# A hybrid convolution and retention block on one core: the MLP's combinations of its second weight moved beside its first product, and modulation products queued behind the rotary of k

## The chip, the cores and the metric

The kernel runs on 1 core of one Trainium2 chip. The metric is the device time of one execution, in microseconds (us).

## The reference

One layer acts on 2048 tokens of width 1024, all in float32. A conditioning vector c gives six vectors of 1024 (shift, scale and gate for either half of the layer).

```
mod = silu(c) @ w_ada + b_ada -> shift1, scale1, gate1, shift2, scale2, gate2
h   = rms_norm(x, g_pre_mix) * (1 + scale1) + shift1
xin, b_gate, c_gate, q, k, v, g = split(h @ w_in)
y_conv = b_gate * causal_conv3(c_gate * xin)
y_ret  = silu(g) * head_norm(retention(rotary(q), rotary(k), v))
x = x + gate1 * rms_norm(concat(y_conv, y_ret) @ w_out, g_post_mix)
h = rms_norm(x, g_pre_mlp) * (1 + scale2) + shift2
f = square(relu(h @ w_fc1)) @ w_fc2
x = x + gate2 * rms_norm(f, g_post_mlp)
```

## The kernel before

**Precision.** Every large product is made of three: both factors are split into a high part, cast by ScalarE, and a low part, subtracted by VectorE, and `mm3` (lines 141 to 144) issues high by high, high by low and low by high into one bank of PSUM.

**The mixer** takes the tokens in four blocks of 512 (b = 0 to 3). In each, `gemm_nat` and `gemm_t` run through the seven parts of `w_in` in the order V, K, G, Q, XIN, C, B and then through `w_out`, with weights of 128x1024 loaded, cast and subtracted by `wgroup` (lines 131 to 139, three buffers). Between them stand the rotary (lines 527 to 544: three VectorE operations on the bank, an addition on GpSimd), the transposes, the retention by tiles of 128 tokens (lines 619 to 660), the convolution, and the normalised input of the MLP of the block before (`h2_prep`). While one block runs, the next block's x is loaded and squared (`h1_scale`, line 238 and line 240) and its input made (`h1_tile`).

**Modulation.** `mod2(gi)` multiplies eight tiles of 128x1024 of `w_ada` (tiles "ada", line 416) by columns of silu(c) and sums them on VectorE into "wide" (lines 418 and 420). It is called for the first gate and the MLP's scale and gate after the part G of blocks 0, 1 and 2, and for the MLP's shift in block 0.

**The MLP** works on two halves of 1024 tokens (B = 0, 1), each product in Winograd's form of Strassen's method: seven products instead of eight, on quarter matrices and their combinations. `fc1` goes through 16 pairs of column tiles (t = 0 to 15, "rounds" below): four quarter weights of 256 KB are loaded (`quads`, line 801), GpSimd makes their four combinations (lines 890 to 893) for the sixth and later products, and seven quarter results leave to DRAM as "fd". `fc2` multiplies them by `w_fc2`, whose four combinations stand in DRAM as "w2d".

**The preparations.** `w2_prep(t)` (lines 496 to 504) makes those combinations for one t: it loads `w2[t]` as two tiles "w2r" of 512 KB (line 499), makes four subtractions in place on GpSimd (line 502) and stores four results of 256 KB (line 504). `w2_some(n)` makes the next n of the 16. It is called at lines 558, 697 and 722, all in the mixer.

**Buffers and order.** The tiles "x", "ada", "w2r", "row" and, in `fc2`, "fw" share one tag of three buffers (`x_tile`, line 86). A scheduler puts the instructions of each engine into one fixed order, which is kept on the chip; `tc.issue_after(i)` adds an edge that queues what is issued inside it behind i on i's engine. All DMAs are issued by SP.

Of the kernel before, what the change touches and what calls it, by code (L numbers as in the profile page):

```python
# [54 lines left out]
def block_kernel(  # L55
# [459 lines left out]
    with pa_stack:  # L515
# [11 lines left out]
        def rotary(ps, coss, sins, t, dst):  # L527
            pv = ps.rearrange("p (h s d) -> p h s d", h=H, s=2)
            qa = tmp()
            nc.vector.tensor_tensor(  # L530
                qa.rearrange("p (x d) -> p x d", d=HALF),
                ps.rearrange("p (x d) -> p x d", d=HALF),
                coss[:, t, :].unsqueeze(1).to_broadcast([P, 2 * H, HALF]),
                op=ALU.mult,
            )
            qb = tmp()
            qbv = qb.rearrange("p (h s d) -> p h s d", h=H, s=2)
            for s in range(2):
                nc.vector.tensor_tensor(
                    qbv[:, :, s, :], pv[:, :, 1 - s, :],  # L540
                    sins[:, t, s, :].unsqueeze(1).to_broadcast([P, H, HALF]),
                    op=ALU.mult,
                )
            nc.gpsimd.tensor_tensor(dst, qa, qb, op=ALU.add)

        for b in range(NB):
# [6 lines left out]
            for ps in vps:  # L553
                v_ = at("va")
                nc.scalar.copy(v_, ps)
                vs.append(v_)
            if b > 0:
                w2_some(2)
            coss, sins = rope_tables(b)
            kds = []  # L560

            def k_end(t, ps):
                kr = tmp()
                rotary(ps, coss, sins, t, kr)
                kd = at("vb")
# [5 lines left out]
                )  # L571
                kds.append(kd)

            if b == 0:
                for t in range(3):
                    k_end(t, kps[t])
                k_end(3, gemm_nat(w_in(KK), h_cur, KS, ALL[3:])[0])
            else:
                for t, ps in enumerate(gemm_nat(w_in(KK), h_cur, KS)):
                    k_end(t, ps)  # L580

# [5 lines left out]
            if b < 3:  # L587
                part = mod2((0, 2, 3)[b])
            kTs = []
# [104 lines left out]
            if b > 0:  # L694
                for _ in h2_prep(b - 1, h2_load(b - 1)):
                    pass
            w2_some(2 if b > 0 else 1)
            for j, ps in enumerate(gemm_t(w_in(BG), h_cur)):
# [13 lines left out]
            for ch, tag in enumerate(("kT", "sg")):  # L712
# [7 lines left out]
                if ch == 0:  # L720
                    if b < NB - 1:
                        w2_some(1)

# [150 lines left out]
    def fc1(B, hl, first, left=None, beside=None):  # L874
# [8 lines left out]
        for t in range(NP):  # L883
# [29 lines left out]
            relu2(f11, f11)  # L913
            nc.sync.dma_start(fd[B][1][t], f11)
            add(f12, prod(6), f12)
            step()
# [257 lines left out]
```

## Time and profile before

| | |
|---|---|
| median of 3 runs | 2238.92 us (2238.62 to 2243.34) |
| profiled execution | 2240.46 us, its span 2238.7 us |
| TensorE (PE), weight loads (PEld) busy | 2143.6 us (96%), 1765.9 us |
| VectorE (DVE), ScalarE (ACT), GpSimd (POOL) busy | 1442.8, 989.9, 586.7 us |
| mean granted TensorE clock | 0.988 |
| moved by DMA | 428.23 MB, mean 191 GB/s |
| loads of w2r | 32 of 512 KB, median 5.4 us to landing |

In the rows, a group of instructions stands with its line, engine, operation and tiles (out<-in, buffer numbers left out); busy time, a mean in ns; an idle time before it with its releaser, the instruction whose end let it go. "SPq" is SP's issuing of DMAs. PEclk is the granted share of TensorE's full clock. Matmuls overlap, so a mean of 390 ns does not say how often one starts. A transfer is busy on 16 DMA engines; "DMA share" is their mean.

### The profile page before, as it was taken

What the parts mean: (1) busy time and instruction counts of PE and PEld (TensorE: products, weight loads), DVE (VectorE), ACT (ScalarE), POOL (GpSimd) and SP (SyncE); (2) the same over time, 40 slices, a digit from 0 to 9 for tenths busy, and PEclk for the clock granted to TensorE, in tenths of its full rate; (3) what the DMA queues carried; (4) which work ended last, traced back from release to release, by engine and by line L of the source; (5) the groups of instructions that cost most, each with busy time, mean ns of one, the idle gap of its engine ahead of it and who ended that gap; (6) DMA issues with size and microseconds to landing.
All of it is one profiled execution on the core that took longest, in us unless ns stands there. A gap on an engine that the chain in (4) does not pass through costs nothing.

```text
span 2238.7 us, 28424 instructions
## 1 busy us (share of the span) xinstructions
PE 2143.6 (96%) x9736; PEld 1765.9 (79%) x9736; DVE 1442.8 (64%) x2198; ACT 989.9 (44%) x1714; POOL 586.7 (26%) x441
## 2 busy tenths in 40 slices
PE   3999999999999999989999999999999999999997
PEld 2787877878787888867888878888888888888885
DVE  7766845675567634776666687556776666555566
ACT  3332532244224522466555556444445555454453
POOL 4132254314423351243333300001433333010012
PEclk8999999999999999999999999999999999999999
DMA  7356467546655563566444477666764443666666
GB/s 283 132 179 220 157 229 242 177 143 214 212 174 202 182 229 129 200 209 217 150 151 148 135 231 219 204 194 192 259 229 155 150 154 120 211 190 197 196 191 242
DMA packets 197426, 428.23 MB, mean 191 GB/s; under 512 B 22560, under 2 KB 22560, under 8 KB 197280
## 3 DMA queue, kind: packets, MB, share of 16 engines
q1 hardware_dynamic: 197280, 426.41, 57.7%
q8 instruction: 76, 1.25, 0.2%
q14 instruction: 70, 0.57, 0.1%
HBM read 322.51 MB, written 103.81 MB: 190 GB/s over the span
## 4 chain that ended last, share of the span: by engine, by line
PE 67%; DMA 11%; issue 10%; DVE 7%; POOL 3%; ACT 1%; SPq 0%; DVEq 0%; POOLq 0%; ACTq 0%
PE g L142 20%; PE g L143 20%; PE g L144 20%; DMA w2r<-in_w 2%; DMA w2d<-w2r 2%; DMA fw<-fd 2%; PE m L142 2%; PE m L143 2%; PE m L144 2%; POOL w2r L502 2%; DMA ada<-in_ada 1%; DMA x<-in_x 1%; DVE pt L199 1%; DVE wl L807 1%; DVE ql L807 1%
## 5 line engine op out<-in xcount | busy, mean ns | idle before, releaser
L143 PE MATMUL g<-ql,wh 128*128 128x512 f32 x896 | 350.9, 392 | 9.6 <-DVE ql L807 9.6
L144 PE MATMUL g<-qh,wl 128*128 128x512 f32 x896 | 350.9, 392 | 0.5 <-DVE wl L807 0.4
L142 PE MATMUL g<-qh,wh 128*128 128x512 f32 x896 | 350.2, 391 | 0.1
L136 ACT CAST whi<-raw 128x1024 fp32r<-128x1024 f32 x148 | 155.3, 1052 | 348.5 <-PE g L144 178.4
L872 DVE TENSOR_TENSOR q<-g,q 128x512 f32<-128x512 f32 x267 | 178.4, 687 | 174.8 <-PE g L144 174.6
L138 DVE TENSOR_TENSOR wlo<-raw,whi 128x1024 fp32r<-128x1024 f32 x140 | 187.6, 1344 | 152.2 <-ACT whi L136 151.7
L807 DVE TENSOR_TENSOR fl<-fw,fh 128x512 fp32r<-128x512 f32 x218 | 161.3, 741 | 162.5 <-ACT fh L806 160.3
L143 PE MATMUL g<-wl,fh 128*128 128x512 f32 x680 | 265.3, 390 | 0.3 <-DVE wl L807 0.3
L144 PE MATMUL g<-wh,fl 128*128 128x512 f32 x680 | 264.6, 389 | 0.0
L806 ACT CAST fh<-fw 128x512 fp32r<-128x512 f32 x218 | 135.2, 620 | 225.8 <-DMA fw<-fd 213.1
L806 ACT CAST wh<-r 128x512 fp32r<-128x512 f32 x224 | 138.8, 620 | 214.7 <-PE g L143 188.7
L142 PE MATMUL g<-wh,fh 128*128 128x512 f32 x680 | 218.4, 390 | 0.8 <-ACT wh L806 0.8
L143 PEld LDWEIGHTS g<-ql,wh 128*128 128x128 f32 x896 | 169.0, 189 | 46.6 <-DVE ql L807 11.5
L144 PEld LDWEIGHTS g<-qh,wl 128*128 128x128 f32 x896 | 169.1, 189 | 36.3 <-DVE wl L807 1.9
L142 PEld LDWEIGHTS g<-qh,wh 128*128 128x128 f32 x896 | 169.3, 189 | 36.1 <-ACT qh L806 0.7
L807 DVE TENSOR_TENSOR wl<-fw,wh 128x512 fp32r<-128x512 f32 x218 | 156.2, 717 | 44.7 <-ACT wh L806 42.2
L1005 POOL TENSOR_TENSOR q<-q,gg 128x512 f32<-128x512 f32 x28 | 43.4, 1577 | 533.4 <-ACT q L1002 285.3
L807 DVE TENSOR_TENSOR wl<-r,wh 128x512 fp32r<-128x512 f32 x224 | 163.6, 731 | 11.0 <-ACT wh L806 10.8
L806 ACT CAST wh<-fw 128x512 fp32r<-128x512 f32 x218 | 135.0, 619 | 65.3 <-PE g L144 30.3
L890 POOL TENSOR_TENSOR r<-r,r 128x512 f32<-128x512 f32 x32 | 41.4, 1294 | 431.8 <-DVE wl L807 384.3
L143 PEld LDWEIGHTS g<-wl,fh 128*128 128x128 f32 x680 | 127.6, 188 | 29.4 <-DVE wl L807 2.9
L142 PEld LDWEIGHTS g<-wh,fh 128*128 128x128 f32 x680 | 127.4, 188 | 28.2 <-ACT wh L806 2.0
(257 smaller groups left out, 4448.6 us busy)
## 6 DMA issues: line engine op xcount, KB each, us to landing
raw<-in_win SPq DMA_DIRECT2D x116, 512.0 KB, 4.2
fd<-q SPq DMA_DIRECT2D x224, 256.0 KB, 2.2
fw<-fd SPq DMA_DIRECT2D x224, 256.0 KB, 2.8
r<-in_w SPq DMA_DIRECT2D x128, 256.0 KB, 4.7
fw<-w2d SPq DMA_DIRECT2D x128, 256.0 KB, 3.0
ada<-in_ada SPq DMA_DIRECT2D x48, 512.0 KB, 4.7
fw<-in_w SPq DMA_DIRECT2D x96, 256.0 KB, 3.6
w2r<-in_w SPq DMA_DIRECT2D x32, 512.0 KB, 5.4
```

The source lines that it names most:

```text
L136: nc.scalar.copy(hi, raw)
L138: (eng or nc.vector).tensor_tensor(lo, raw, hi.bitcast(F32), op=ALU.subtract)
L142: nc.tensor.matmul(ps, ah, bh, start=first, stop=False)
L143: nc.tensor.matmul(ps, ah, bl, start=False, stop=False)
L144: nc.tensor.matmul(ps, al, bh, start=False, stop=last)
L199: nc.vector.scalar_tensor_tensor(pt, raw[:, k, :], c_, pt, op0=ALU.mult, op1=ALU.add)
L502: nc.gpsimd.tensor_tensor(o, a, b_, op=ALU.subtract)
L806: nc.scalar.copy(hi, src)
L807: nc.vector.tensor_tensor(lo, src, hi.bitcast(F32), op=SUB)
L872: (eng or nc.vector).tensor_tensor(o, a, b_, op=ADD)
L890: nc.gpsimd.tensor_tensor(b11, b12, b11, op=SUB)
L1005: eng.tensor_tensor(c, c, gg[1][:, j * 512 : j * 512 + 512], op=ALU.mult)
```

## The change

All three calls of `w2_some` in the mixer go. `fc1` calls it instead, in half 0 alone, after the store of the second product's result: one preparation in rounds 1 to 14 and two in round 15. And `rotary` returns its last VectorE instruction, `k_end` passes it on, and `mod2` after the part G is issued behind that of the fourth token tile.

```diff
--- before.py
+++ after.py
@@ -536,12 +536,13 @@
             qb = tmp()
             qbv = qb.rearrange("p (h s d) -> p h s d", h=H, s=2)
             for s in range(2):
-                nc.vector.tensor_tensor(
+                ins = nc.vector.tensor_tensor(
                     qbv[:, :, s, :], pv[:, :, 1 - s, :],
                     sins[:, t, s, :].unsqueeze(1).to_broadcast([P, H, HALF]),
                     op=ALU.mult,
                 )
             nc.gpsimd.tensor_tensor(dst, qa, qb, op=ALU.add)
+            return ins
 
         for b in range(NB):
 
@@ -554,14 +555,12 @@
                 v_ = at("va")
                 nc.scalar.copy(v_, ps)
                 vs.append(v_)
-            if b > 0:
-                w2_some(2)
             coss, sins = rope_tables(b)
             kds = []
 
             def k_end(t, ps):
                 kr = tmp()
-                rotary(ps, coss, sins, t, kr)
+                k_last = rotary(ps, coss, sins, t, kr)
                 kd = at("vb")
                 nc.gpsimd.tensor_tensor(
                     kd.rearrange("p (h d) -> p h d", h=H),
@@ -570,14 +569,15 @@
                     op=ALU.mult,
                 )
                 kds.append(kd)
+                return k_last
 
             if b == 0:
                 for t in range(3):
                     k_end(t, kps[t])
-                k_end(3, gemm_nat(w_in(KK), h_cur, KS, ALL[3:])[0])
+                k_last = k_end(3, gemm_nat(w_in(KK), h_cur, KS, ALL[3:])[0])
             else:
                 for t, ps in enumerate(gemm_nat(w_in(KK), h_cur, KS)):
-                    k_end(t, ps)
+                    k_last = k_end(t, ps)
 
             sgs = []
             for ps in gemm_nat(w_in(GG), h_cur, KS):
@@ -585,7 +585,8 @@
                 nc.scalar.activation(sg, ps, AF.Silu)
                 sgs.append(sg)
             if b < 3:
-                part = mod2((0, 2, 3)[b])
+                with tc.issue_after(k_last.ins):
+                    part = mod2((0, 2, 3)[b])
             kTs = []
             for t in range(NT):
                 tps = mbank()
@@ -694,7 +695,6 @@
             if b > 0:
                 for _ in h2_prep(b - 1, h2_load(b - 1)):
                     pass
-            w2_some(2 if b > 0 else 1)
             for j, ps in enumerate(gemm_t(w_in(BG), h_cur)):
                 y = tmp()
                 nc.vector.tensor_tensor(y, ps, cc[j], op=ALU.mult)
@@ -718,8 +718,6 @@
                     ms.append(m)
                 mixs.append(ms)
                 if ch == 0:
-                    if b < NB - 1:
-                        w2_some(1)
 
                     if b + 1 < NB:
                         rb = spread(r1)
@@ -912,6 +910,8 @@
             step()
             relu2(f11, f11)
             nc.sync.dma_start(fd[B][1][t], f11)
+            if left is not None and t > 0:
+                w2_some(1 if t < NP - 1 else 2)
             add(f12, prod(6), f12)
             step()
             f22 = q(t, "kT")
```

The scheduler then orders every engine anew. **VectorE in block 1, the rotary of k** (line 530 and line 539 make a token tile's two products with the cosines and sines, lines 418 and 420 are modulation products, line 138 the low part of a weight). Before:

```order
L530 TENSOR_TENSOR tmp_2688<-g_2563,coss_2561 128x512
L539 TENSOR_TENSOR tmp_2690<-g_2563,sins_2556 128x4x64 x2
L418 TENSOR_SCALAR wide_2855<-ada_2856,sc 128x1024
L530 TENSOR_TENSOR tmp_2697<-g_2564,coss_2561 128x512
L539 TENSOR_TENSOR tmp_2699<-g_2564,sins_2556 128x4x64 x2
L138 TENSOR_TENSOR wlo_2791<-raw_2787,whi_2789 128x1024
L530 TENSOR_TENSOR tmp_2706<-g_2565,coss_2561 128x512
L539 TENSOR_TENSOR tmp_2708<-g_2565,sins_2556 128x4x64 x2
L420 SCALAR_TENSOR_TENSOR wide_2855<-ada_2859,sc,wide_2855 128x1024
L530 TENSOR_TENSOR tmp_2715<-g_2566,coss_2561 128x512
L539 TENSOR_TENSOR tmp_2717<-g_2566,sins_2556 128x4x64 x2
L420 SCALAR_TENSOR_TENSOR wide_2855<-ada_2862,sc,wide_2855 128x1024
```

With the change:

```order
L530 TENSOR_TENSOR tmp_2640<-g_2515,coss_2513 128x512
L539 TENSOR_TENSOR tmp_2642<-g_2515,sins_2508 128x4x64 x2
L530 TENSOR_TENSOR tmp_2649<-g_2516,coss_2513 128x512
L539 TENSOR_TENSOR tmp_2651<-g_2516,sins_2508 128x4x64 x2
L530 TENSOR_TENSOR tmp_2658<-g_2517,coss_2513 128x512
L539 TENSOR_TENSOR tmp_2660<-g_2517,sins_2508 128x4x64 x2
L138 TENSOR_TENSOR wlo_2743<-raw_2739,whi_2741 128x1024
L530 TENSOR_TENSOR tmp_2667<-g_2518,coss_2513 128x512
L539 TENSOR_TENSOR tmp_2669<-g_2518,sins_2508 128x4x64 x2
L418 TENSOR_SCALAR wide_2807<-ada_2808,sc 128x1024
L420 SCALAR_TENSOR_TENSOR wide_2807<-ada_2811,sc,wide_2807 128x1024
```

The modulation's products stood between the tiles of the rotary; now all four tiles come first.

**SP in the same place** (w2d and w2r belong to preparations, raw are weights). Before:

```order
L504 DMA w2d_2_703<-w2r_2503 128x512
L499 DMA w2r_2514<-in_w 128x1024
L134 DMA raw_2787<-in_win 128x1024
L499 DMA w2r_2515<-in_w 128x1024
L504 DMA w2d_3_656<-w2r_2514 128x512
L134 DMA raw_2817<-in_win 128x1024
L504 DMA w2d_3_688<-w2r_2514 128x512
L504 DMA w2d_3_672<-w2r_2515 128x512
L416 DMA ada_2856<-in_ada 128x1024
L504 DMA w2d_3_704<-w2r_2515 128x512
L134 DMA raw_2912<-in_win 128x1024
L416 DMA ada_2859<-in_ada 128x1024
```

With the change (lines below 558 stand one to three numbers lower or higher in the new file; L744 is the store that was L746):

```order
L744 DMA x1d_606<-sg_2284 128x512
L416 DMA ada_2808<-in_ada 128x1024
L744 DMA x1d_607<-kT_2059 128x512
L744 DMA x1d_607<-sg_2288 128x512
L416 DMA ada_2811<-in_ada 128x1024
L134 DMA raw_2679<-in_win 128x1024
L134 DMA raw_2709<-in_win 128x1024
L134 DMA raw_2739<-in_win 128x1024
L134 DMA raw_2769<-in_win 128x1024
L134 DMA raw_2864<-in_win 128x1024
L134 DMA raw_2894<-in_win 128x1024
```

The stores that wait for GpSimd and the loads of w2r are gone from between the weights, and the first two loads of ada stand ahead of them.

**SP in the first product of the MLP, half 0, from the end of round 3** (fd are its results, L799 the quarter weights). With the change:

```order
L504 DMA w2d_4_689<-w2r_9333 128x512
L952 DMA fd_7_3_7866<-q_9094 128x512
L504 DMA w2d_5_658<-w2r_9511 128x512
L954 DMA fd_5_3_7882<-q_8937 128x512
L504 DMA w2d_4_673<-w2r_9334 128x512
L957 DMA fd_6_3_7850<-q_9099 128x512
L499 DMA w2r_9512<-in_w 128x1024
L960 DMA fd_3_3_7898<-q_9102 128x512
L504 DMA w2d_4_705<-w2r_9334 128x512
L912 DMA fd_1_4_7819<-q_9114 128x512
L504 DMA w2d_5_690<-w2r_9511 128x512
L499 DMA w2r_9689<-in_w 128x1024
```

Before, only the fd rows and the loads of quarter weights stood here. Now a load of a w2r half is followed by stores of earlier combinations, and the results of the round stand between them. The 16 preparations stand in SP's order from shortly before the first result of round 1 to the middle of round 10, ahead of the rounds in which they are called.

**GpSimd in the same place** (L888 to L891 are the quarter weights' combinations of round 4, lines 890 to 893 before). With the change:

```order
L888 TENSOR_TENSOR r_9105<-r_9107,r_9105 128x512
L502 TENSOR_TENSOR w2r_9333<-w2r_9334,w2r_9333 128x512
L889 TENSOR_TENSOR r_9167<-r_9111,r_9105 128x512
L890 TENSOR_TENSOR r_9107<-r_9111,r_9107 128x512
L502 TENSOR_TENSOR w2r_9511<-w2r_9511 128x512
L502 TENSOR_TENSOR w2r_9334<-w2r_9334,w2r_9333 128x512
L891 TENSOR_TENSOR r_9109<-r_9109,r_9167 128x512
L502 TENSOR_TENSOR w2r_9334<-w2r_9334 128x512
L502 TENSOR_TENSOR w2r_9511<-w2r_9512,w2r_9511 128x512
L502 TENSOR_TENSOR w2r_9512<-w2r_9512,w2r_9511 128x512
L502 TENSOR_TENSOR w2r_9512<-w2r_9512 128x512
```

The preparations' subtractions stand between the four of a round, which stood alone before.

## Rows read from the trace of the kernel before

**Rows 1.** Table of stretches: us, busy (instructions) by engine, PEclk, DMA share, GB/s.

```profile
380.00:410.00 30.00, 26.28 (x116) 20.79 (x115) 9.86 (x19) 12.31 (x25) 13.49 (x12) 0.94 0.72 242
1050.00:1300.00 250.00, 250.00 (x1105) 207.01 (x1104) 164.75 (x240) 130.03 (x214) 79.41 (x52) 1.00 0.44 147
540.00:560.00 20.00, 20.00 (x90) 16.57 (x89) 5.62 (x6) 6.77 (x10) 9.36 (x7) 1.00 0.87 303
1550.00:1600.00 50.00, 50.00 (x223) 41.40 (x222) 35.53 (x57) 24.44 (x46) 9.30 (x8) 1.00 0.81 276
```

**Rows 2.** TensorE's waits from 318, 380, 555, 770, 196, 655 us: us, times, longest.

```profile
PE g L142 <- DVE tmp L539: 3.5, 1, 3.5
PE g L143 <- DVE wlo L138: 1.2, 1, 1.2
...
PE g L142 <- ACT whi L136: 2.7, 1, 2.7
PE g L144 <- DVE wlo L138: 1.1, 2, 0.5
...
PE g L142 <- DVE tmp L539: 1.8, 1, 1.8
PE g L143 <- DVE wlo L138: 1.1, 1, 1.1
...
PE g L143 <- DVE wlo L138: 1.5, 1, 1.5
...
PE m L631 <- DVE sg L655: 3.0, 1, 3.0
...
PE m L644 <- DVE sg L655: 1.9, 1, 1.9
```

**Rows 3.** SP's waits, whole run: us, times, longest.

```profile
SPq L504 <- POOL w2r L502: 94.1, 54, 6.0
SPq L238 <- DMA w2d<-w2r: 12.5, 6, 4.5
```

**Rows 4.** Time line of VectorE, block 1: start, us, what [idle before].

```profile
332.83 0.76 DVE L418 TENSOR_SCALAR wide<-ada,sc 128x1024 f32<-128x1024 f32 x1 [7.88 <-DMA ada<-in_ada]
```

**Rows 5.** Time line of ScalarE, block 1.

```profile
384.50 0.63 ACT L240 ACTIVATE junk<-x 128x512 f32<-128x512 f32 x1 [12.73 <-DMA x<-in_x]
...
393.71 0.63 ACT L240 ACTIVATE junk<-x 128x512 f32<-128x512 f32 x1 [2.32 <-DMA x<-in_x]
```

**Rows 6.** Chain that ended last, block 2: start, us, what.

```profile
554.90 5.39 DMA w2r<-in_w
...
564.24 4.01 DMA ada<-in_ada
```

**Rows 7.** Time line of SP, first product of the MLP, half 0.

```profile
1053.16 1.82 SPq L801 DMA_DIRECT2D r<-in_w  x4
...
1072.20 1.82 SPq L801 DMA_DIRECT2D r<-in_w  x4
```

**Rows 8.** Chain that ended last, block 1.

```profile
357.02 4.36 DMA w2r<-in_w
...
371.44 4.01 DMA w2r<-in_w
```

**Rows 9.** Groups of GpSimd, whole run.

```profile
L502 POOL TENSOR_TENSOR w2r<-w2r 128x512 f32<-128x512 f32 x32 | 44.3, 1383 | 131.5 <-DMA w2r<-in_w 73.2 <-DVE wide L420 44.8 <-DVE wlo L138 12.3
```

**Rows 10.** Time line of ScalarE, first product of the MLP, half 0.

```profile
1068.91 0.62 ACT L806 CAST wh<-r 128x512 fp32r<-128x512 f32 x1 [2.04 <-PE g L143]
```

**Rows 11.** Line 801, the quarter weights' loads, from 1050 to 1300 us.

```profile
DMA to landing us min/median/max: 3.6/4.6/6.1
```

**Rows 12.** Groups of VectorE from 1050 to 1300 us.

```profile
L951 DVE TENSOR_TENSOR q<-q,q 128x512 f32<-128x512 f32 x13 | 14.8, 1135 | 6.4 <-ACT q L877 6.4
L953 DVE TENSOR_TENSOR q<-q,q 128x512 f32<-128x512 f32 x13 | 9.0, 692 | 0.4
```

## The prediction

> **What bounds the kernel now.** I read the table of stretches first, then TensorE's waits, then SP's waits, and last the time lines at the places found. In the first product of the MLP, half 0, TensorE is busy for all 250 us of the stretch shown, while the DMA engines are busy 0.44 of it and move 147 GB/s [rows 1]. Nothing beside TensorE can be saved there; something can only be lost. In the mixer (up to about 980 us) TensorE does wait, and each wait has a place. In block 1 it waits 3.5 us for the rotary of k, 1.2 us for a weight's low part, and 2.7 us and 1.1 us for a weight's high and low part; in block 2, 1.8 us for the rotary and 1.1 us for a low part; in block 3, 1.5 us for a low part; in the retention of blocks 0 and 2, 3.0 us and 1.9 us for the evictions at line 655 [rows 2]. Around 395 us the granted clock also falls: 0.94 over 30 us [rows 1], so 0.06 x 30 = 1.8 us. Together 19.6 us.
>
> What ends these waits? SP issues all transfers in one order. Its stores of the combinations waited 94.1 us for GpSimd, and its loads of x waited 12.5 us for those stores, since w2r, x and ada share three buffers of one tag [rows 3]. VectorE sat 7.88 us in front of the first product of a modulation for its ada tile, with the rotary queued behind it [rows 4]: that is the 3.5 us. ScalarE sat 12.73 us and 2.32 us in front of squares of x that had landed late [rows 5], and the cast that TensorE missed for 2.7 us is queued behind the second. The squares also stand ahead of the retention's square (line 649), which feeds line 655.
>
> **The change part by part.** *Gone from the mixer:* 16 preparations, each two loads of 512 KB, four subtractions on GpSimd and four stores of 256 KB. SP then has no row in the mixer that waits for GpSimd's subtractions, and x and ada find their buffers free. What this touches is 1.2 + 1.1 + 1.5 us of late weights, 2.7 + 1.1 us behind late x, 3.0 + 1.9 us in the retention and the 1.8 us of clock: 14.3 us.
>
> *Moved behind the rotary of k:* the eight products of blocks 0 to 2. The wait in [rows 4] can no longer hold the rotary: 3.5 + 1.8 = 5.3 us. What is late next are the splits of the weights behind the products. A product waits for a load that needs a buffer freed by the product three before; one such load took 4.01 us [rows 6]. If one landing per block shows, this gives back 12 us; if the three loads ahead cover it, nothing. In the new order the first two ada loads of block 1 stand ahead of six loads of weights and so come early, which is nearer to the covered end: I take 2 us.
>
> Of the 19.6 us I subtract these 2 us and a quarter of the rest of the first part (3.6 us) for waits that will show only once the first ones are gone: **14 us gained**, with ends 5 us (the rotary alone, the rest replaced) and 20 us.
>
> *Added in the first product of the MLP, half 0:* the same 16 preparations. In SP's new order they run from shortly before round t = 1 to about the middle of round 10, so 9.5 rounds. A round is 19.04 us, from one load of four quarter weights to the next [rows 7], so TensorE offers 9.5 x 19.04 = 181 us, or 11.3 us for each preparation. Three things must fit into that.
>
> First, the chain: the second half of a weight loads, GpSimd makes the second combination from it, this is stored, and its landing frees the buffer for the next second half. In block 2 one such link took from 554.90 to 564.24, 9.3 us [rows 6]; in block 1, with more subtractions in it, 357.02 to 371.44, 14.4 us [rows 8]. Times 16: 149 or 231 us.
>
> Second, the traffic: 16 x 2.1 MB = 33.6 MB on top of 147 GB/s x 181 us = 26.6 MB, 60.2 MB. The fastest longer stretches were 303 GB/s over 20 us and 276 GB/s over 50 us [rows 1]: 199 or 218 us, 18 or 37 us later than TensorE would like. Neither stretch had its DMA engines fully busy (0.87 and 0.81), so neither is a ceiling. The Trainium skill (DMA: Bandwidth & Descriptors, Specifications) gives about 358 GB/s as a core's share of HBM; by it, as an estimate, 60.2 MB take 168 us and this term would be nothing. No stretch read here comes near that rate.
>
> Third, GpSimd: 64 subtractions at 1.38 us [rows 9] are 88 us beside four per round of its own, and they stand between these in its order, so a late w2r load holds the sixth product's weight.
>
> What covers lateness: a quarter weight was loaded at 1053.16 and its first cast began at 1068.91; with a median landing of 4.6 us this leaves 11 us [rows 7, 10, 11]. GpSimd's own results are wanted sooner: the weight buffers are three deep, two products of 12 matmuls at 250 / 1105 = 0.226 us are 5.4 us, less the split's some 1.4 us: 4 us. So a chain near the first link (149 us) costs nothing; 199 us costs 18 - 11 = 7 us or 18 - 4 = 14 us; 218 us costs 26 to 33 us. The stretch at 303 GB/s is the nearest row, but it was not full, so I go below its 7 us: **5 us lost**, ends 0 and 33 us.
>
> The sum is 14 - 5 = **9 us faster**. The profiled execution took 2240.46 us (span 2238.7); the median of the runs shown is 2238.92 us, 1.5 us below it, so 2231.5 us there and about **2230 us** as a median.
>
> **The rivals.**
>
> *The queue falls behind (slower).* SP's order is fixed, so once stores of combinations are late, the next quarter weights are issued late. For it: 60.2 MB in 181 us are 332 GB/s and neither stretch in [rows 1] held that; a link of 14.4 us was seen. Against it: the short link is under the 11.3 us wanted, and the stretches in [rows 1] left DMA engines idle. It decides from the point where lateness exceeds cover and gain, 11 + 14 = 25 us, that is 12.9 us per preparation. At 218 us: 26 - 14 = 12 us slower, 2251 us; at 231 us: 39 - 14 = 25 us slower, 2264 us.
>
> *The mixer's waits come back (no change).* Gain 5 us, loss 5 us: 2239 us. For it: after each named wait TensorE depends on the same three weight buffers and on products that wait for loads. Against it: the lateness of x and of the weights has one source in [rows 3], and it leaves.
>
> *GpSimd holds VectorE (slower).* VectorE's subtraction at line 951 took 1135 ns in this stretch where line 953, of the same shape, took 692 [rows 12]. Against 64 more GpSimd operations this is 64 x 0.44 = 28 us on top of VectorE's 165 of 250 us, 119 of 181: 147 us, which fits. If each held VectorE for its full 1.38 us, it would be 119 + 88 = 207 us, 26 us over, less the 14 gained: 2251 us. The Trainium skill (SBUF — State Buffer, Who interferes with whom) says that a VectorE operation with two SBUF inputs and a GpSimd operation that reads SBUF exclude each other, and the later one waits for the whole of the other. What [rows 12] show is a partial wait only.
>
> That the change does not do what it says is excluded by the new order, which has the products behind all four rotaries and no preparation in the mixer.
>
> **How the numbers follow.** A measurement of this kernel can tell about 0.2%, 4.5 us, from no change. Forecast (5 to 20 us faster): 0.56. Waits come back: 0.20, all within 0.2%. Queue falls behind: 0.20, of which 0.03 within 0.2%, 0.16 slower and 0.01 still faster. VectorE held: 0.04, slower. So faster 0.57, same 0.23, slower 0.20. The best bound, 20 us gained and nothing lost, is 2219 us, and the link may do a little better: low end 2216 us. The upper end takes in waits that come back and the queue at 218 us up to 2250 us; the rest of that rival and of the held VectorE, some 0.12, is left out, and 0.05 below.
>
> **What would show it.** Right: TensorE's waits for the rotary (line 539) in blocks 1 and 2 gone, as are those for evictions in the retention of block 0; SP without waits for w2d stores before 980 us; the mixer some 14 us shorter; the first product, half 0, within about 5 us of its length, at 300 GB/s or more in its first ten rounds. Wrong: TensorE waiting in rounds 3 to 10 for the split of a quarter weight, or for GpSimd's differences, round lengths of 21 us or more there, or products on VectorE in the mixer with splits waiting behind them.

## The result and the profile after

The changed kernel took 2243.30 us (median of 22 runs, 2238.16 to 2250.76), the kernel before 2237.74 us beside it (22 runs): ratio 1.0024, interval 1.0015 to 1.0034. It is 5.6 us **slower**, where 9 us faster were forecast. The one profiled execution of the changed kernel took 2238.93 us (span 2236.8), near the fast end of its runs, and that of the kernel before 2240.46 us, so the two profiles stand 1.5 us apart the other way round: the changed kernel's is 4 us under its median, the other 2.7 us over its own. They are read here for where time goes, stage by stage, and the medians for how much there is of it.

Line numbers below 558 moved a little: the splits of line 807 stand at line 805 after the change, the evictions of line 872 at 870, GpSimd's four combinations (890 to 893) at 888 to 891; the four results that end a round keep lines 951 to 959.

The table of stretches (us, then busy time and count of PE, PEld, DVE, ACT, POOL, then PEclk, DMA share, GB/s), first one of the kernel before, then two of the changed kernel:

```profile
250.00:500.00 250.00, 239.57 (x1149) 198.07 (x1148) 158.94 (x266) 92.09 (x168) 81.98 (x63) 0.99 0.58 194
```

```profile
250.00:500.00 250.00, 247.96 (x1199) 206.98 (x1199) 162.81 (x266) 97.62 (x177) 53.60 (x43) 1.00 0.49 159
...
1050.00:1300.00 250.00, 232.79 (x999) 188.13 (x998) 185.49 (x218) 113.53 (x193) 141.53 (x95) 0.99 0.70 237
```

In this part of the mixer TensorE sits idle for 2 us of 250, where it was 10 us before. In the first product of the MLP, where it was busy for all of 250 us [rows 1], it lacks 17 us, and VectorE is busy for longer, 185.49 us for 164.75, with fewer operations, 218 for 240. A follower of both kernels is VectorE's first operation of the four that end a round (s3, line 951). It came at 1010.0 us in round 0 before and at 981.8 us after: a lead of **28 us** out of the mixer. In round 15 it came at 1307.6 and 1306.6 us: 1 us is left. From round 1 to round 15 it took 269.1 us before and 295.2 us after, so **26 us are lost** in fourteen rounds, and the first nine of them lose it: 19.9, 23.1, 22.4, 19.7, 23.6, 26.7, 21.7, 21.6 and 21.1 us, then 16.7, and from there on 19.0, 19.0, 21.4 and 19.1, as before.

TensorE's waits of the changed kernel from 50 to 1310 us (us, times, longest):

```profile
PE g L144 <- DVE wl L805: 17.1, 11, 3.3
PE g L143 <- DVE ql L805: 9.4, 3, 8.3
PE g L142 <- ACT wh L804: 5.2, 3, 3.6
PE g L142 <- DVE tmp L539: 3.3, 2, 2.9
```

The second stands in front of the MLP in both kernels, and of the fourth 2.9 us is the rotary of block 0, where it was 2.7 us before. The first and the third are new and lie in the first product: 22.3 us for the low or the high part of a quarter weight. The granted clock was 0.91, not 1.00, in two stretches of 19 us (1050 to 1069 and 1145 to 1164 us), in each behind a wait, of 2.2 and 3.6 us; that is 1.7 us each. Together 25.7 us, of which 2.5 us (at 983 and 994 us) lie ahead of the run of round 1: some 23 of the 26 us.

**One round on VectorE.** Its time line before, at the end of a round (start, us, what):

```profile
1075.19 0.91 DVE L807 TENSOR_TENSOR wl<-r,wh 128x512 fp32r<-128x512 f32 x1
1076.64 1.16 DVE L951 TENSOR_TENSOR q<-q,q 128x512 f32<-128x512 f32 x1 [0.54 <-ACT q L877]
1077.83 0.69 DVE L953 TENSOR_TENSOR q<-q,q 128x512 f32<-128x512 f32 x1
1078.44 0.68 DVE L807 TENSOR_TENSOR wl<-r,wh 128x512 fp32r<-128x512 f32 x1
1079.04 0.68 DVE L956 TENSOR_TENSOR q<-q,q 128x512 f32<-128x512 f32 x1
1079.76 0.69 DVE L959 TENSOR_TENSOR q<-q,q 128x512 f32<-128x512 f32 x1
1080.37 0.68 DVE L872 TENSOR_TENSOR q<-g,q 128x512 f32<-128x512 f32 x1
1080.97 0.68 DVE L807 TENSOR_TENSOR wl<-r,wh 128x512 fp32r<-128x512 f32 x1
```

And after, with GpSimd beside it:

```profile
1053.37 1.11 DVE L805 TENSOR_TENSOR wl<-r,wh 128x512 fp32r<-128x512 f32 x1 [3.05 <-ACT wh L804]
1054.40 1.78 DVE L951 TENSOR_TENSOR q<-q,q 128x512 f32<-128x512 f32 x1
1056.11 1.77 DVE L805 TENSOR_TENSOR wl<-r,wh 128x512 fp32r<-128x512 f32 x1
1057.81 1.78 DVE L953 TENSOR_TENSOR q<-q,q 128x512 f32<-128x512 f32 x1
1059.62 1.67 DVE L956 TENSOR_TENSOR q<-q,q 128x512 f32<-128x512 f32 x1
1061.21 0.68 DVE L870 TENSOR_TENSOR q<-g,q 128x512 f32<-128x512 f32 x1
1061.81 0.68 DVE L959 TENSOR_TENSOR q<-q,q 128x512 f32<-128x512 f32 x1
1062.41 0.68 DVE L805 TENSOR_TENSOR wl<-r,wh 128x512 fp32r<-128x512 f32 x1
```

```profile
1047.18 1.29 POOL L502 TENSOR_TENSOR w2r<-w2r 128x512 f32<-128x512 f32 x1 [6.20 <-DMA w2d<-w2r]
1048.43 1.74 POOL L888 TENSOR_TENSOR r<-r,r 128x512 f32<-128x512 f32 x1
1050.14 1.29 POOL L502 TENSOR_TENSOR w2r<-w2r,w2r 128x512 f32<-128x512 f32 x1
1051.38 1.30 POOL L889 TENSOR_TENSOR r<-r,r 128x512 f32<-128x512 f32 x1
1052.63 1.30 POOL L890 TENSOR_TENSOR r<-r,r 128x512 f32<-128x512 f32 x1
1053.88 1.76 POOL L502 TENSOR_TENSOR w2r<-w2r 128x512 f32<-128x512 f32 x1
1055.59 1.75 POOL L502 TENSOR_TENSOR w2r<-w2r,w2r 128x512 f32<-128x512 f32 x1
1057.29 1.75 POOL L891 TENSOR_TENSOR r<-r,r 128x512 f32<-128x512 f32 x1
1059.00 1.74 POOL L502 TENSOR_TENSOR w2r<-w2r 128x512 f32<-128x512 f32 x1
```

Two things can be seen. **The run at the round's end** (the sixth product's low part, lines 951, 953, 956 and 959 and the next low part between them, called the run below): before, one operation starts 0.60 us after the other, and the next product's low part starts 5.8 us behind the first. After, they start every 1.70 us while GpSimd works, each 0.5 us behind the start of one of GpSimd's, which take 1.70 us too instead of 1.25: the engines take turns, and the same stretch lasts 9.0 us. At 1059.00 GpSimd begins its last subtraction here, and VectorE is then back at 0.60 us. Line 870 has one input in PSUM and is not held: from 1000 to 1290 us it ran 24 times wholly inside operations of GpSimd, at 0.68 to 0.69 us. One of these, from the end of the round before (VectorE's row, then GpSimd's, which are two subtractions):

```profile
1038.09 0.68 DVE L870 TENSOR_TENSOR q<-g,q 128x512 f32<-128x512 f32 x1
```

```profile
1035.89 3.42 POOL L502 TENSOR_TENSOR w2r<-w2r,w2r 128x512 f32<-128x512 f32 x2
```

**The start of GpSimd's own four:** line 888 writes over a tile that VectorE reads for the first product's low part, so it could start when that was made, at 1046.07 us. It stands behind a subtraction that waited for its tile until 1047.18, starts 2.4 us late, and another subtraction stands between lines 888 and 889, on whose result the sixth product's split waits. That split's low part comes 7.3 us behind the point at which line 888 could have started; before, 4.2 us. ScalarE's waits from 1010 to 1215 us (us, times, longest) show the same wait, which the kernel before has nowhere in that stretch:

```profile
ACT wh L804 <- POOL r L889: 27.7, 9, 6.9
```

No cast and no low part of a quarter weight waits for its load there: the loads were issued in time, although SP waited 39.7 us for GpSimd's subtractions in front of stores.

So there were three suspects when the experiments began: the traffic, the turns that VectorE and GpSimd take (the lock, below), and GpSimd's fixed order (the queue).

### The profile page after: what moved, and what is told of

It is laid out like the page before. It is cut to its first block, busy times and chain, and to the rows that moved or that the text cites. A ratio compares the mean times of both kernels' runs of the same rounds, so it can differ in the third digit from the quotient of the medians.

```text
span 2236.8 us, 28404 instructions
## 1 busy us (share of the span) xinstructions
PE 2139.7 (96%) x9736; PEld 1763.5 (79%) x9736; DVE 1484.5 (66%) x2198; ACT 986.8 (44%) x1714; POOL 591.4 (26%) x441
## 3 DMA queue, kind: packets, MB, share of 16 engines
q8 instruction: 76, 1.25, 0.2%
## 5 line engine op out<-in xcount | busy, mean ns | idle before, releaser
L805 DVE TENSOR_TENSOR wl<-r,wh 128x512 fp32r<-128x512 f32 x224 | 189.9, 849 | 41.5 <-ACT wh L804 40.7
L144 PEld LDWEIGHTS g<-qh,wl 128*128 128x128 f32 x896 | 169.5, 189 | 59.8 <-DVE wl L805 24.9
L144 PEld LDWEIGHTS g<-wh,fl 128*128 128x128 f32 x680 | 127.6, 188 | 26.3
```

The lines of the kernel that those rows point to most:

```text
L144: nc.tensor.matmul(ps, al, bh, start=False, stop=last)
L805: nc.vector.tensor_tensor(lo, src, hi.bitcast(F32), op=SUB)
```

## The experiments

All results at a glance. "Ratio" is to the kernel before beside it, whose median was 2239.34 us beside runs 1 to 4, 2237.59 beside 5 to 8, 2237.53 beside 9 and 10, and 2237.47 beside 11 and 12; "lead" is how much earlier than in the profile of before (1010.0 us) the run of round 0 came; "rounds" is the time from the run of round 1 to that of round 15.

| run | median, us | ratio (interval) | lead, us | rounds, us |
|---|---|---|---|---|
| before | 2237.74 | | 0 | 269.1 |
| after | 2243.30 | 1.0024 (1.0015 to 1.0034) | 28.3 | 295.2 |
| 1 preparations moved alone | 2248.39 | 1.0046 (1.0032 to 1.0060) | 21.0 | 295.7 |
| 2 modulation queued alone | 2231.86 | 0.9968 (0.9956 to 0.9980) | 6.2 | 268.7 |
| 3 traffic alone | 2211.87 | 0.9882 (0.9869 to 0.9894) | 24.9 | 264.8 |
| 4 subtractions on VectorE | 2219.86 | 0.9917 (0.9904 to 0.9929) | 26.5 | 272.6 |
| 5 work alone | 2243.03 | 1.0023 (1.0012 to 1.0033) | 9.3 | 280.4 |
| 6 behind the run | 2242.63 | 1.0022 (1.0011 to 1.0033) | 19.7 | 267.2 |
| 7 in the run | 2229.36 | 0.9970 (0.9956 to 0.9983) | 23.3 | 279.8 |
| 8 mixer, traffic alone | 2231.71 | 0.9974 (0.9964 to 0.9985) | 4.5 | 269.1 |
| 9 six behind the run | 2234.93 | 0.9988 (0.9978 to 0.9999) | 28.2 | 293.1 |
| 10 mixer, loads alone | 2227.77 | 0.9947 (0.9933 to 0.9960) | 14.0 | 268.9 |
| 11 four and twelve | 2212.41 | 0.9889 (0.9873 to 0.9906) | 25.0 | 269.4 |
| 12 mixer, copies in DRAM | 2210.57 | 0.9884 (0.9869 to 0.9899) | 27.1 | 268.7 |

Leads come from one profile each and lie between 19.7 and 28.3 us for one and the same mixer (the changed kernel, 3, 4, 6, 7 and 9); rounds differ by chance far less. In run 3 the run of round 1 stands 4 us later in its round, so its 264.8 us stand for 269. A check that does not depend on the run: from the first product's first matmul to the second product's first, TensorE took 326.2 us before, 353.6 after, 325.0 in run 2, 324.8 in run 3, 333.9 in run 5, 349.4 in run 6, 335.1 in run 7, 349.0 in run 9 and 324.8 in run 11.

**1 and 2. The two parts apart.** From the changed kernel, and from the one before (beside it, as in the change, `rotary` and `k_end` hand their last instruction on):

```diff
-                with tc.issue_after(k_last.ins):
-                    part = mod2((0, 2, 3)[b])
+                part = mod2((0, 2, 3)[b])
```

```diff
-                part = mod2((0, 2, 3)[b])
+                with tc.issue_after(k_last.ins):
+                    part = mod2((0, 2, 3)[b])
```

> The preparations move into the MLP's first product, the modulation products are not queued behind the rotary. Theory A (the lost time lies in the first product of the MLP alone, and the mixer gains from the preparations' going): the mixer is still over 15 us shorter than in the kernel before, of the 28 us that the whole change gains there; rounds 2 to 10 again take 20 to 27 us where they took 19.04; time 2240 to 2250 us, about that of the whole change. Theory B (the gain in the mixer is the rotary's): the mixer gains under 10 us, and the time is 2255 us or more.

> The modulation products are queued behind the rotary of k, the preparations stay in the mixer. Theory A: TensorE's waits for line 539 (8.0 us) become small, a part comes back as waits for late weights; 2232 to 2237 us, with rounds of 19.04 us in the MLP. Theory B: most of the mixer's 28 us is gained by this alone, about 2215 us. A third case is no gain at all (2238 us): the products then wait for their late tiles behind the rotary and hold the splits of the weights.

Measured: 2248.39 and 2231.86 us. Theory A holds in both (run 2 is 0.1 us below its range). The queueing of the modulation alone is worth 7.5 us; the move of the preparations alone costs 9 us, although its mixer leads by 21.0 us. Leads add up: 21.0 + 6.2 = 27.2, of 28.3.

**3 and 4. The subtractions left out, or on VectorE.**

```diff
-        for o, a, b_ in ((c11, c12, c11), (c12, c22, c12), (c22, c22, c11), (c21, c21, c22)):
+        for o, a, b_ in ():
```

```diff
-            nc.gpsimd.tensor_tensor(o, a, b_, op=ALU.subtract)
+            nc.vector.tensor_tensor(o, a, b_, op=ALU.subtract)
```

> The changed kernel without the preparations' 64 subtractions: their 32 loads and 64 stores remain in the MLP's first product, with the same bytes, and what is stored is the weight itself, so the output is not the reference's. Lock theory (GpSimd's subtractions and VectorE's operations on two SBUF tiles take turns at 1.70 us for a pair, and VectorE's results come late): rounds 2 to 10 go back to 19.04 us within 0.3, VectorE's low part at line 805 from 963 ns back to about 720 ns, and the time falls by about 26 us to 2214 to 2222 us. Queue theory (late stores and loads in SP's order delay the quarter weights): the traffic is the same, rounds stay at 21 us or more, and the time stays above 2235 us.

> The changed kernel with the 64 subtractions on VectorE instead of GpSimd. Lock theory: a subtraction takes about 0.7 us there (44 us over some ten rounds, on an engine that was busy 165 of 250 us), nothing alternates with GpSimd but its own four combinations of a round, and rounds 2 to 10 take 19.0 to 20 us; 2216 to 2228 us. Queue theory: as slow as the changed kernel, 2238 us or more. A third case: VectorE waits in its fixed order for loads of w2r that land late, and TensorE waits for the low parts behind them; rounds of 20 to 23 us, 2230 to 2245 us.

Measured: 2211.87 us, 2 us below the range of the lock theory, and 2219.86 us, within it. The table of stretches and VectorE's groups from 1050 to 1210 us, first of the changed kernel, then of the traffic alone:

```profile
1050.00:1210.00 160.00, 142.79 (x602) 113.60 (x601) 121.34 (x127) 65.75 (x114) 114.40 (x78) 0.98 0.84 280
...
L805 DVE TENSOR_TENSOR wl<-r,wh 128x512 fp32r<-128x512 f32 x49 | 50.7, 1035 | 25.5 <-ACT wh L804 25.1
...
L953 DVE TENSOR_TENSOR q<-q,q 128x512 f32<-128x512 f32 x7 | 12.3, 1759 | 0.0
```

```profile
1050.00:1210.00 160.00, 160.00 (x708) 132.53 (x707) 104.11 (x153) 82.32 (x135) 49.54 (x33) 1.00 0.88 309
...
L805 DVE TENSOR_TENSOR wl<-r,wh 128x512 fp32r<-128x512 f32 x59 | 42.1, 714 | 0.0
...
L953 DVE TENSOR_TENSOR q<-q,q 128x512 f32<-128x512 f32 x9 | 6.2, 692 | 0.3
```

The same bytes moved at 309 GB/s, faster than in the changed kernel, and TensorE was busy for all 160 us: **the traffic costs nothing**, and the queue of SP does not fall behind. It was the subtractions. (In this run no store waits for GpSimd; that such waits did not delay the quarter weights in the changed kernel either is shown by ScalarE's waits above.) On VectorE they cost some 8 us over the traffic alone (seven rounds of 19.2 to 21.4 us, with low parts behind them), the third case in part; still 20 us faster than the kernel before. What these two runs can't tell is the lock from GpSimd's queue: both go with the subtractions.

**5, 6 and 7. Place against place.** Run 7 paces the preparations, one a round, directly behind line 891 (first diff); run 5 does the same subtractions there, on two tiles that are loaded once, with the preparations left in the mixer (second); run 6 holds them behind the last of VectorE's run by a copy of one column (third). The diffs show the lines that matter. In all three the call of the changed kernel goes.

```diff
+                    last_[0] = nc.gpsimd.tensor_tensor(b21, b21, t2, op=SUB)
...
             add(f12, prod(6), f12)
+            if left is not None and t > 0:
+                with tc.issue_after(last_[0].ins):
+                    w2_some(1 if t < NP - 1 else 2)
```

```diff
+                    w2_idle(1 if t < NP - 1 else 2)
...
+        for _ in range(n):
+            c11, c12, c21, c22 = (c[:, i : i + 512] for c in idle for i in (0, 512))
+            for o, a, b_ in ((c11, c12, c11), (c12, c22, c12), (c22, c22, c11), (c21, c21, c22)):
+                nc.gpsimd.tensor_tensor(o, a, b_, op=ALU.subtract)
```

```diff
             nc.sync.dma_start(fd[B][3][t], s4)
+            if left is not None and t > 0:
+                gate = small([P, 1], "gate")
+                g_ = nc.gpsimd.tensor_copy(gate, s4[:, 0:1])
+                with tc.issue_after(g_.ins):
+                    w2_some(1 if t < NP - 1 else 2)
```

> The preparations stay in the mixer as before, the modulation is queued behind the rotary (as in the second run), and in addition 64 subtractions of the same shape run on GpSimd in the MLP's first product, four a round directly behind the last of GpSimd's own four (line 891 of the changed kernel), on two tiles loaded once: no traffic is added and nothing waits for their results. Lock theory: they fall into the stretch in which VectorE makes the four results from two tiles each, each holds one VectorE operation for about 1.1 us, and of the 4.4 us a round 1 to 2.5 us reach TensorE: rounds of 20 to 21.5 us, 14 to 35 us in all, 2246 to 2267 us against 2232 us without them. Queue theory: GpSimd has time for them and nothing is stored, rounds of 19.04 us, 2232 us.

> The changed kernel with the same preparations on GpSimd, one in each round 1 to 14 and two in round 15, held back by a copy of one column of VectorE's last result of the round (s4), so that the four subtractions start when VectorE's run of two-tile operations is over. Lock theory: each subtraction then meets one low part (line 805) in a product of 2.72 us in which VectorE is busy for half the time, so that the wait is covered: rounds of 19.04 us within 0.3, and 2210 to 2220 us, as with traffic alone. A theory by which any subtraction on GpSimd costs its time, wherever it stands: 64 x 1.1 = 70 us of waits are left on VectorE, rounds of 20 us or more and 2228 us or more. Queue theory: the traffic is spread over more rounds, with some gain, 2225 to 2238 us.

> The pair to the run behind the burst: the same preparations at the same pace of one a round, but with their subtractions directly behind GpSimd's own last combination of the round (line 891), so where VectorE makes its run of two-tile operations. Lock theory: rounds of 20 to 21.5 us as with the work alone, so 2226 to 2248 us, at least 10 us above the run behind the burst. If pace alone decides (one preparation a round where the changed kernel runs 1.7), this one is as fast as that: 2210 to 2220 us.

Measured: 2243.03, 2242.63 and 2229.36 us. In runs 5 and 7 nearly every round takes 19.6 us, with traffic or without: the run stretches from 5.8 to 10.1 us, line 888 starts on time (0.08 us behind its release, as before), and only 0.55 us of the 4 reach TensorE. **The lock alone** is real, but smaller than the 1 to 2.5 us a round that were expected. In run 6 it is gone, and every round from the second on takes 19.04 us, the mechanism as foretold. GpSimd's time line there:

```profile
1088.10 1.30 POOL L888 TENSOR_TENSOR r<-r,r 128x512 f32<-128x512 f32 x1 [3.40 <-DVE wl L805]
...
1092.49 1.75 POOL L891 TENSOR_TENSOR r<-r,r 128x512 f32<-128x512 f32 x1
1097.52 0.18 POOL L961 COPY gate<-q 128x1 f32<-128x1 f32 x1 [3.27 <-DVE q L957]
1097.65 1.29 POOL L502 TENSOR_TENSOR w2r<-w2r 128x512 f32<-128x512 f32 x1
1099.03 3.33 POOL L502 TENSOR_TENSOR w2r<-w2r,w2r 128x512 f32<-128x512 f32 x2
```

Its time was wrong all the same, and so was the gap of 10 us to run 7, for a reason outside both theories. TensorE's time line behind the last round:

```profile
1305.77 2.07 PE L142 MATMUL g<-wh,fh 128*128 128x512 f32 x4 [23.83 <-ACT wh L804]
```

And SP's in front of it:

```profile
1288.83 4.61 SPq L504 DMA_DIRECT2D w2d<-w2r  x4
...
1296.85 0.37 SPq L499 DMA_DIRECT2D w2r<-in_w  x1
...
1299.75 0.32 SPq L975 DMA_DIRECT2D fw<-fd  x1
```

The second product's first load (line 975) stands behind the stores and the last load of the two preparations of round 15, whose tiles are of the tag that it shares. In runs 5 and 7 the run of round 15 comes 6 us later in its round, since splits of the second product stand before it in VectorE's order. Little of that reaches TensorE: up to the second product run 5 takes 8.9 us longer than run 2 and run 7 10.3 us longer than run 3, and 14 x 0.55 = 7.7 us of it is the lock.

**8. The mixer's side.** Run 2 with the loop of run 3 left out in the mixer:

> On the mixer's side: the kernel of the second run (preparations in the mixer, modulation behind the rotary) without the 64 subtractions; the loads and stores remain in the mixer, with the same bytes, and what is stored is the weight itself, so the output is not the reference's. If the subtractions (stores that wait for them in SP's order, buffers that come free late, VectorE held by GpSimd) were what the mixer lost by the preparations: TensorE's waits in the mixer fall to those of the changed kernel, and 2210 to 2220 us. If it was the traffic and the three shared buffers: 2228 to 2234 us, no change against the second run.

Measured: 2231.71 us against 2231.86 us of run 2. In the mixer the subtractions, and what stores wait for GpSimd alone, cost nothing; the traffic or what it holds costs all. The stores still wait in SP's order here, 73.7 us in 32 waits up to 980 us, now for the loads of w2r.

**9. Six a round.** Run 6 with `w2_some` cut into single subtractions, each store behind those that it needs, and six subtractions behind each copy, so that the preparations end in round 11:

```diff
                 with tc.issue_after(g_.ins):
-                    w2_some(1 if t < NP - 1 else 2)
+                    for _ in range(6):
+                        next(w2_todo, None)
```

> The run behind the burst with one thing changed: six subtractions a round instead of four (from round 1 on), so that the last preparation is through in round 11 instead of round 15. Theory: what that run lost, it lost only behind the last round, where the two preparations of round 15 held the tiles and the place in SP's order that the first loads of the second product want (TensorE waited 23.8 us there at once); six subtractions take 8 to 9 us of the 9.6 us between VectorE's run and GpSimd's own next combination. Then rounds of 19.04 us, no wait at the second product's start, and 2210 to 2217 us, faster than both kernels and than the subtractions on VectorE (2219.9 us). Rival: six do not fit before GpSimd's next combination, so that the sixth product's split is late; rounds of 19.5 to 21 us and 2218 to 2235 us.

Measured: 2234.93 us; the rival holds, and with rounds of 20.2 to 24.1 us more strongly than it said. GpSimd's time line:

```profile
1098.63 1.29 POOL L503 TENSOR_TENSOR w2r<-w2r 128x512 f32<-128x512 f32 x1
...
1105.55 1.73 POOL L503 TENSOR_TENSOR w2r<-w2r 128x512 f32<-128x512 f32 x1
1110.70 1.28 POOL L503 TENSOR_TENSOR w2r<-w2r,w2r 128x512 f32<-128x512 f32 x1 [3.41 <-DMA w2r<-in_w]
1111.94 1.29 POOL L888 TENSOR_TENSOR r<-r,r 128x512 f32<-128x512 f32 x1
```

The miss is worth more than a hit: it is **the queue alone**. VectorE's run is undisturbed (6.0 us, median of ten rounds), but GpSimd waits 3.41 us for a load with line 888 behind it, line 888 starts 3.2 to 7.6 us late in the weights of rounds 3 to 12, and the fourteen rounds take 293.1 us, nearly as long as in the changed kernel. Both the waits for loads (up to 3.7 us) and the time of the subtractions themselves stand in front of line 888; this run does not part the two.

**10 and 12. What the mixer lost.** Run 8 with the stores moved into the MLP's first product (from the tile f11); and run 2 with copies from the weight straight to w2d in DRAM, queued behind the load of a weight traced just before:

```diff
-        for i, a in ((5, c11), (7, c12), (6, c22), (4, c21)):
-            nc.sync.dma_start(w2d[i][t], a)
...
             nc.sync.dma_start(fd[B][1][t], f11)
+            if left is not None:
+                for i in (5, 7, 6, 4):
+                    nc.sync.dma_start(w2d[i][t], f11)
```

```diff
-        halves = [x_tile("w2r") for _ in range(2)]
...
+        with tc.issue_after(raw_last[0].ins):
+            for n, i in enumerate((5, 7, 6, 4)):
+                nc.sync.dma_start(w2d[i][t], w2[t][:, n * 512 : n * 512 + 512])
```

> The pair to the run with the preparations' traffic in the mixer (2231.7 us): there the 32 loads of w2r alone remain, still in the three shared buffers, no subtractions, and the 64 stores are made in the MLP's first product from another tile, so the output is not the reference's. If the mixer loses by SP's order, which stops at each store until its data is there (71 us of SP's waits in that run), the loads alone cost little: TensorE's waits in the mixer near those of the changed kernel, and 2210 to 2220 us. If it loses by the loads themselves (the shared buffers and the bytes): 2225 to 2232 us, no change against that run.

> On the mixer's side, a third step beside its traffic run (2231.7 us) and its loads alone (2227.8 us): in the mixer, at the places of the preparations, 64 copies of 256 KB straight from the second weight to the places of its combinations in DRAM. As many bytes are read and written, but no tile is held, no store waits for a load in SP's order and nothing is subtracted, so the output is not the reference's. If the three shared buffers and SP's waiting stores are what blocks 1 and 2 lost: 2210 to 2218 us, as without preparations. If it is the bytes themselves, in a mixer that moves about 195 GB/s on average with stretches near 300: 2226 to 2234 us.

Measured: 2227.77 and 2210.57 us. The copies cost nothing, so the bytes were not it. SP's waits from 230 to 690 us with the loads alone:

```profile
SPq L499 <- DMA w2r<-in_w: 23.8, 10, 4.2
...
SPq L416 <- DMA w2r<-in_w: 9.2, 4, 3.2
SPq L738 <- DMA w2r<-in_w: 7.8, 3, 4.4
SPq L238 <- DMA w2r<-in_w: 7.8, 3, 3.5
```

Loads of w2r, ada and x wait in SP's one order for a tile that an earlier load of w2r still fills, and weights stand behind them. By medians, the loads cost 2227.8 - 2210.6 = 17 us, the stores 4 us more (2231.7), the subtractions nothing.

**11. The version that follows.** Four preparations stay in the mixer's block 3, the interval that gained least (TensorE's idle time between the retentions of blocks 2 and 3 fell from 5.4 to 2.1 us); twelve stand in rounds 1 to 12 behind the copy of run 6:

```diff
+            if b == NB - 1:
+                w2_some(2)
             coss, sins = rope_tables(b)
...
+            if b == NB - 1:
+                w2_some(2)
             for j, ps in enumerate(gemm_t(w_in(BG), h_cur)):
...
+                with tc.issue_after(g_.ins):
+                    w2_some(1)
```

> The version that the runs point to: four preparations stay in the mixer's block 3, where the whole change gained nothing (222.1 us before, 222.2 us after, between the retentions of blocks 2 and 3), and twelve go into the MLP's first product, one a round in rounds 1 to 12, held behind VectorE's run of two-tile operations as in the run behind the burst; the modulation is queued behind the rotary. Theory (GpSimd's place in the round and a free start of the second product are all that counts): rounds of 19.04 us, no wait of 20 us at the second product's start, the mixer's lead of some 25 us kept: 2208 to 2217 us, as with traffic alone (2211.9 us), and faster than the subtractions on VectorE. Rival: block 3 loses now what blocks 1 and 2 lost before, 4 of 16 preparations, some 5 us: 2217 to 2222 us.

Measured: 2212.41 us, 25 us under the kernel before (ratio 0.9889) and 31 us under the changed one by their medians. Rounds of 19.04 us from the second to the end of the twelve, line 888 on time, the run 5.79 us.

## Why the prediction was wrong

**The direction was wrong because the loss in the first product was put at 5 us and is 26 us in the profile, 31 us by the medians of the changed kernel and run 3.** The gain in the mixer was put at 14 us and is some 27 (run 3 against the 2239.34 us beside it: 27.5), which by itself would only have made the change better. With the profile's 26 us the two all but cancel; that the median is slower rests on the 31.

*The step that failed first* is the third of the "three things" that must fit, GpSimd. The text said that the subtractions stand between its own four, "so a late w2r load holds the sixth product's weight", and gave it 4 us of cover. Then it priced lateness by totals over the stretch, of the chain and of the traffic, as if a load could be late only when all are. In the changed kernel GpSimd waits up to 6.6 us for a single preparation's tile, and the subtractions behind the wait stand in front of line 888, which starts 1.1 to 6.7 us late in six of the rounds 4 to 11 (0.08 us before). The cover itself was about right: in run 9 a low part of the sixth product that came 3.4 us later behind the release of line 888 than before (7.5 for 4.2 us) cost TensorE 0.3 us, one that came 5.0 us later 1.7 us. Run 9 shows the queue alone at 24 us in fourteen rounds; run 3 shows that the traffic, at 309 GB/s, is worth 0.

*The step that failed second* is the rival "GpSimd holds VectorE", given 0.04. Its mechanism was right: the turns at 1.70 us. It was refused by a sum over the stretch (VectorE 147 us of 181, "which fits"), but the turns fall where VectorE has six operations in a row with no idle time, and there the run takes 9 to 11 us for 5.8. [Rows 12] showed it: the 1135 ns of line 951 were one such turn at each round's end, read as "a partial wait only". The Trainium skill (SBUF — State Buffer, Who interferes with whom) gives the exclusion for two SBUF inputs and none for an operation with one. The trace agrees, with 1.78 us for line 951 against 0.68 us for line 870 beside the same work of GpSimd. Alone the lock costs 0.55 us a round (runs 5 and 7). From the release of line 888 to the next low part behind the run it is 9.96 us before, 13.95 in run 7, so the cover there is 4.0 - 0.55 = 3.4 us. In the changed kernel these stretches last 14.0 to 20.9 us in the weights of rounds 2 to 10, and what they exceed 9.96 + 3.4 us by adds up to 24 us: the lock eats the cover, and what GpSimd's queue adds is then paid in full. TensorE's waits stand accordingly: 14.4 us at the low part right behind the run and 7.0 us at the sixth product's split, where run 9, with VectorE's run undisturbed, has 2.4 and 10.4 us.

*"The queue falls behind"* (0.20) gave the right sign and nearly the time (2251 us), by the wrong cause. Run 3 and run 12 take the traffic out of it in both places.

*The gain in the mixer* was right in its causes and too small. Between the retentions of block 0 and block 3 TensorE was idle for 23.0 us before (10.0, 7.6 and 5.4 us by blocks) and for 4.5 us after. The list in the prediction looked into chosen stretches and found 14.8 us of these 23; and nothing came back of the 3.6 and 2 us that were taken off "for waits that will show only once the first ones are gone" and for the queued products. That "the lateness of x and of the weights has one source in [rows 3], and it leaves" holds, but the source is the w2r loads in the shared tiles (17 us) rather than the stores that wait for GpSimd (54 waits, 94.1 us of SP's time): with the subtractions gone nothing was gained (run 8, where the stores wait for loads instead), and with the stores gone too only 4 us (run 10).

*The rotary's 5.3 us* are worth 7.5 us alone (run 2): TensorE's waits for line 539 in blocks 1 and 2 fell from 3.5 and 1.8 us to 0 and 0.3. *The mixer's waits come back* did not happen. What the forecast named as a sign of being wrong, TensorE waiting in rounds 3 to 10 for the split of a quarter weight and rounds of 21 us or more, is what the trace shows.

One thing stays open: the profiled execution of the changed kernel is 4 us faster than its median, and where the slower executions lose more, so the 5 us between 26 and 31, was not traced.

## What to carry to other kernels

Work that moves to an engine with time to spare is not free there: ask what stands behind it in that engine's fixed order, and whether what it waits for can come late in a single round, since an average over the stretch hides both. Where VectorE has a run of operations on two SBUF tiles, put GpSimd's work behind its end; a copy of one column of the run's last result does that, at 0.18 us a round here. Put no more there than is done before the engine's next urgent work: four subtractions a round cost nothing, six cost 24 us in fourteen rounds (runs 11 and 9). And let moved work end well before a stage that needs its buffers.

## What the runs showed of the hardware

VectorE and GpSimd, each with two SBUF tiles of 128x512 in float32, took turns at 1.70 us for a pair (the changed kernel, runs 5 and 7), where alone they start every 0.60 and 1.25 us; VectorE's operations with one input in PSUM kept 0.68 us beside the same GpSimd work. A rate of 309 GB/s over 160 us, with the DMA engines busy for 0.88 of it, left every quarter weight in time (run 3). And 64 copies of 256 KB from DRAM to DRAM in the mixer cost nothing that can be measured beside a mixer without preparations (2210.57 against 2211.87 us of run 3), where the same bytes by way of three shared tiles cost 21 us (run 8, 2231.71 us).
